# The sixteen gate columns move into the first head's v group, which becomes the second group of the input projection; side streams pause once instead of twice, and a head's loads are issued while the head before it still runs

## The chip, the core and the metric

The kernel runs on one core of a Trainium2 chip. The metric is device time in microseconds (us). The engines are named as in the profile: PE (TensorE), PEld (its weight loads), DVE (VectorE), ACT (ScalarE), POOL (GpSimd), SP (SyncE, which only issues DMAs here). L69 is line 69 of the kernel before.

## The reference, cut to what matters

One encoder block on 512 tokens of width 2048. The first projection feeds two branches, and the sixteen columns `g` of it are the gates of the second branch.

```python
hn = rmsnorm(x, norm1_w[l])
proj = hn @ w_in[l]                              # 2048 -> 11280 columns
conv_out = centred_depthwise_conv(proj[..., :5120], ...)
rest = proj[..., 5120:]
hv, hx1, hx2 = ...                               # 3 x 1024 columns: the hyena branch
z   = hx1 * long_conv(hv, kf[:, 0], hb[0])
y_a = hx2 * long_conv(z, kf[:, 1], hb[1])
q, k = silu(conv_out[..., 3072:])                # 4 heads of 256
v = rest[..., :1024]                             # columns 5120..6143
o = sigmoid(rest[..., 1024:2048])
g = rest[..., 2048:2064] + mlstm_gate_bias[l]    # 16 columns: 4 gates x 4 heads
y_b = o * (mlstm(q, k, v, g forward) + mlstm(q, k, v, g backward))
x = x + (gate_a * (y_a @ w_branch_a) + gate_b * (y_b @ w_branch_b)) @ w_out
x = x + (silu(gate) * up) @ w_down               # the feed-forward part, then a last rmsnorm
```

## The kernel before, in words

Every fp32 product is made of three TensorE passes (`mm3`, L69): an operand is split into a high and a low part (`wh`/`wl` for weights, `a` for the normalised input, `g` for tiles of the side work), by a cast on ACT (L169 for weights) and a subtraction on DVE (L170).

The part that the change touches is the first 840 us or so. It is a **main stream** with **side streams** woven into it. The main stream multiplies the input by `w_in` in groups of 256 columns: a group is 16 blocks of 128 rows, taken two at a time (a unit, 12 matmuls of 512 columns or 24 of 256), and after every unit the generator yields (a tick). Weights come by SP in pieces of four blocks (`load_a`, three buffers); the class `Weights` splits them two units ahead. A q, k or hyena group holds two PSUM banks of the pool `mm` (four banks), a v group (`group_v`) holds all four, since there the input stands still in the array and the weights stream through.

The order of groups in the main stream is written out: the first hyena group; then `gate_cols`, the sixteen gate columns as a group of their own; then the hyena's second and third kinds, hyena part 1, head 0 (q, k, v), hyena parts 2 and 3, heads 1 to 3, and four groups `o`. `gate_cols` puts the gate weights into a 128-column tile `wg` (most of it zero), multiplies it with the input, adds the bias in rows (`gb`) and turns the result by four small matmuls against `csm` into token-major `gates`.

At each tick `drive` gives the side streams 2.6 units of cost, about one for each us of DVE work. `turns` goes round the streams; a stream that yields "pause" is skipped until two ticks later (PAUSE = 2), and one that yields "wait" has nothing to do yet. Stream b makes the filter network and eight filter spectra, then the combinations `T` for the next phase. Stream a starts with `gate_rows` (gate arithmetic on small tiles `gs`), then does hyena 0 and 1, head 0, hyena 2 and 3 and heads 1 to 3 (`mlstm`). A head loads q and k (POOL queue), splits them, makes four score tiles (S, 24 matmuls of 512 columns, evicted by ACT at L861), loads v and a row of decays, and then makes weights on ACT, POOL (`affine_select`, L898) and DVE (L900, L904) for the matmuls `num` of 258 columns. All tiles `g` come from one pool of 24 buffers.

The order of instructions on each engine is then set by a scheduling layer from its own estimates; each engine works its list off in that order.

After this phase come the Winograd groups (tiles `T`), the branches, the output projection and the feed-forward part; the change does not touch their code.

Of the kernel before, what the change touches and what calls it, by code (L numbers as in the profile page):

```python
# [8 lines left out]
F32 = mybir.dt.float32  # L9
# [25 lines left out]
def hybrid_block_kernel(ctx, tc, x, norm1_w, w_in, conv_w, conv_b, filt_w1, filt_b1, filt_freq1,  # L35
# [26 lines left out]
    def mm_ps():  # L62
        return new(pm, "mm")

    def sd_ps():
        return new(psd, "sd")
# [14 lines left out]
        return h, l  # L81


    csm = new(cp, "csm", (P, 3 * P + 16))
    nc.sync.dma_start(csm[:, 0:P], c_small[:, 0:P])
    ident = csm[:, 0:P]
    triu = csm[:, P:2 * P]
    tril = csm[:, 2 * P:3 * P]
    sel32 = csm[0:32, 3 * P:3 * P + 16]
    onesf = new(cp, "onesf", (P, P))  # L90
    nc.vector.memset(onesf, 1.0)

# [63 lines left out]
        return bc  # L156


    def load_a(w, r0, c0, nk=4, ncol=256):
        n_tile[0] += 1  # L160
        raw = wpool[0].tile([P, nk, ncol], F32, tag="wr", name=f"wr_{n_tile[0]}", bufs=3)
        nc.sync.dma_start(raw, w[r0:r0 + nk * P, c0:c0 + ncol].rearrange("(k p) c -> p k c", p=P))
        return raw

    def split_w(src, shape):
# [7 lines left out]
    class Weights:  # L173
# [6 lines left out]
        def get(self, c0, kb):  # L180
            assert self.units[self.given] == (c0, kb)
            while len(self.made) < min(self.given + 1 + self.ahead, len(self.units)):
                uc, uk = self.units[len(self.made)]
                if uk % 4 == 0:
                    self.raw = load_a(w_in, uk * P, uc)
# [211 lines left out]
    def head_cols(h):  # L397
        for base, blk0, dst in ((C_Q, 24, d_q), (C_K, 32, d_k)):
            for r in group_feat(w_in, 0, KB, base + h * 256, X, ahead=ahead):
                if r is None:  # L400
                    yield
            for j in range(2):
                conv_evac(r[j], blk0 + 2 * h + j, False, store_to(dst[2 * h + j]))
        later.append((0, lambda: done.add(("qk", h))))
        for r in group_v(w_in, C_V + h * 256, X, ahead):
            if r is None:
                yield
        for tb in range(4):
# [3 lines left out]
        done.add(("v", h))  # L412

    def o_cols(g):
        for r in group_feat(w_in, 0, KB, C_O + g * 256, X, ahead=ahead):
# [9 lines left out]
    a_col = new(cp, "a_col", (P, 2, 4, 4))  # L425
    em_col = new(cp, "em_col", (P, 2, 4, 4))

    gates_t = []

    def gate_cols():  # L430
        gps = mm_ps()
        for u in range(0, KB, 4):
            raw = load_a(w_in, u * P, C_G, 4, 16)
            n_tile[0] += 1
            g = wp.tile([P, 4, P], F32R, tag="wh", name=f"wg_{n_tile[0]}", bufs=4)
            nc.vector.memset(g.bitcast(F32), 0.0)
# [7 lines left out]
        gb = new(cp, "gb", (32, 1))  # L444
        nc.vector.memset(gb, 0.0)
        nc.gpsimd.dma_start(gb[0:16], mlstm_gate_bias[0].rearrange("g h -> (g h)").rearrange("(n o) -> n o", o=1))
        gT = gt()
        nc.vector.tensor_tensor(gT[0:32], gps[0:32], rbc[0:32], ALU.mult)
        nc.vector.tensor_scalar(gT[0:32], gT[0:32], gb, None, ALU.add)
        ps = sd_ps()  # L450
        for tb in range(4):
            mm(ps[:, tb * 16:(tb + 1) * 16], gT[0:32, tb * P:(tb + 1) * P], sel32, True, True)
        gates = new(cp, "gates", (P, 4, 2, 2, 4))
        gates_t.append(gates)
        nc.vector.tensor_copy(gates.rearrange("p a b c d -> p (a b c d)"), ps[:, 0:64])
        done.add("gates matmul")

    def gate_rows():
        yield from need("gates matmul")
        gates = gates_t[0]  # L460

        n = [0]

        def sm(shape=(P, 32)):
            n[0] += 1
            return pr.tile(list(shape), F32, tag=f"gs{n[0]}", name=f"gs{n[0]}", bufs=1)

        f = sm()
        nc.vector.tensor_copy(f.rearrange("p (d t h) -> p t d h", d=2, t=4), gates[:, :, :, 1, :])
# [76 lines left out]
    def filter_net():  # L546
# [16 lines left out]
        nc.sync.dma_start(csm[:, P:3 * P + 16], c_small[:, P:3 * P + 16])  # L563
        yield "pause"
        for m, t in enumerate(tables):
            hh = new(ph, f"dH{m}", dt=F32R)
# [160 lines left out]
    def conv_long(q, o, halves, finish):  # L727
# [45 lines left out]
        for half in range(2):  # L773
# [7 lines left out]
            finish(half, ps)  # L781
            yield 1.4

    def hyena(q):
        yield from need(("hy", q))

        def load(kind):
            ts = []
            for j in range(2):
                t = gt()  # L790
                nc.gpsimd.dma_start(t, d_hy[kind][2 * q + j])
                ts.append(t)
            return ts

        u = load(0)
        x1 = load(1)
        yield "pause"
        halves = []
        for ps in by_times(u):
# [3 lines left out]
        for ps in by_times(x1):  # L803
            t = gt()
            nc.scalar.copy(t, ps)
            x1t.append(t)
        yield "pause"
        z = []

        def gate(half, ps):  # L810
# [2 lines left out]
            z.append(gsplit(t))  # L813

        yield from conv_long(q, 0, halves, gate)
        x2 = load(2)
        y = []

        def keep(half, ps):
# [1 line left out]
            nc.scalar.copy(t, ps)  # L821
            y.append(t)

        yield "pause"
        yield from conv_long(q, 1, z, keep)
        yield "pause"
        for j in range(2):
# [7 lines left out]
            yield 1.1  # L835


    def mlstm(h):
        yield from need("gates")
        yield from need(("qk", h))  # L840
        qs, ks = [], []
# [6 lines left out]
        yield "pause"  # L848
        for dst in (qs, ks):
            for j in range(2):  # L850
                dst.append(gsplit(raw.pop(0)))
                yield .7
        yield "pause"
        S = []
        for sb in range(4):
# [5 lines left out]
            nc.scalar.activation(t, ps, AF.Copy, scale=1.0 / 16)  # L861
            S.append(t)
            yield .3
        yield from need(("v", h))

        def load_row(d):
            t = gt()
            nc.gpsimd.dma_start(t, d_rows[4 * d + h:4 * d + h + 1].to_broadcast([P, L]))
            return t

        V = []
        raw = []
        for b in range(2):
            t = gt()
            nc.gpsimd.dma_start(t.rearrange("p (b c) -> p b c", b=2),
                                d_v[h][2 * b:2 * b + 2].rearrange("b p c -> p b c"))
            raw.append(t)
        row = load_row(0)
        yield "pause"
# [34 lines left out]
        for n, (d, jb) in enumerate(units):  # L914
            if n == 4:
                W = {}
            W[jb] = nxt
            if n < 7:
                nxt = weights(*units[n + 1], row if n < 3 else row_b)
# [30 lines left out]
            yield "wait"  # L950

    def stream_a():
        yield from gate_rows()
        yield from need("filter")
        for kind, n in (("hy", 0), ("hy", 1), ("hd", 0), ("hy", 2), ("hy", 3)):
            yield from hyena(n) if kind == "hy" else mlstm(n)
        ph_cm.__exit__(None, None, None)
        ts_pool.append(ts_cm.__enter__())
        done.add("ts")
        for h in (1, 2, 3):  # L960
            yield from mlstm(h)

    def stream_b():
        yield from filter_net()
# [162 lines left out]
    N_PLAIN = 4  # L1127
    AHEAD = 2
    RATIO = 2.6
    side = turns(stream_b(), stream_a())  # L1130

    parts = (("hy", 1), ("hd", 0), ("hy", 2), ("hy", 3), ("hd", 1), ("hd", 2), ("hd", 3))
    groups = [HW, 2 * HW]
    for kind, n in parts:
        groups += [b + 256 * n for b in ((0, HW, 2 * HW) if kind == "hy" else (C_Q, C_K, C_V))]
# [403 lines left out]
```

## Time and profile before

| | us |
|---|---|
| median of 3 runs (lowest, highest) | 2893.85 (2893.14, 2894.86) |
| time of the profiled execution | 2894.33 |
| its span, first to last instruction | 2892.3 |
| PE busy over the span | 2864.4 |
| DVE busy over the span | 2107.2 |
| ACT busy over the span | 1274.4 |
| mean granted TensorE clock | 0.998 |

A row of the timeline gives the start, the duration, the engine, the line, the operation with its output and inputs, and how many were merged; a bracket gives idle time before it and what ended it. Matmuls overlap in that view (their ends are modelled), so the cost of one in a row of many is the distance from start to start, and the chain view, which gives each piece only the time that it adds, shows the same. A row of the waits gives who waited for whom, the sum, how often, and the longest.

### The profile page before, as it was taken

What the parts mean: (1) busy time and instruction counts of PE and PEld (TensorE: products, weight loads), DVE (VectorE), ACT (ScalarE), POOL (GpSimd) and SP (SyncE); (2) the same over time, 40 slices, a digit from 0 to 9 for tenths busy, and PEclk for the clock granted to TensorE, in tenths of its full rate; (3) what the DMA queues carried; (4) which work ended last, traced back from release to release, by engine and by line L of the source; (5) the groups of instructions that cost most, each with busy time, mean ns of one, the idle gap of its engine ahead of it and who ended that gap; (6) DMA issues with size and microseconds to landing.
All of it is one profiled execution on the core that took longest, in us unless ns stands there. A gap on an engine that the chain in (4) does not pass through costs nothing.

```text
span 2892.3 us, 48200 instructions
## 1 busy us (share of the span) xinstructions
PE 2864.4 (99%) x18412; PEld 2592.2 (90%) x18412; DVE 2107.2 (73%) x3844; ACT 1274.4 (44%) x2267; POOL 185.7 (6%) x431
## 2 busy tenths in 40 slices
PE   9999999999999999999999999999999999999998
PEld 7788887898889999888899999999999998888886
DVE  7897977889588888454549888888888985233336
ACT  5434354436565455222435444444444445233224
POOL 0101011102210001000110000000000000000000
PEclk9999999999999999999999999999999999999999
DMA  5334334334444444743443433343343336343333
GB/s 179 121 108 130 117 117 141 111 106 143 149 136 128 135 140 138 245 139 95 152 148 109 129 121 114 120 126 118 117 128 114 118 110 207 96 130 117 124 113 127
DMA packets 285589, 377.01 MB, mean 130 GB/s; under 512 B 18620, under 2 KB 222852, under 8 KB 285357
## 3 DMA queue, kind: packets, MB, share of 16 engines
q1 hardware_dynamic: 261339, 298.36, 33.4%
q0 software_dynamic: 22752, 73.44, 7.5%
q8 instruction: 144, 2.36, 0.3%
q10 hardware_dynamic: 1266, 2.13, 0.2%
q14 instruction: 88, 0.72, 0.1%
HBM read 326.67 MB, written 47.20 MB: 129 GB/s over the span
## 4 chain that ended last, share of the span: by engine, by line
PE 94%; DVE 3%; DMA 2%; issue 1%; ACT 1%; SPq 0%; POOL 0%; DVEq 0%; ACTq 0%; POOLq 0%
PE mm L69 67%; PE sd L69 26%; DMA bt<-d_o 1%; DMA wr<-in_w_down_dram 0%; DVE wl L170 0%; DVE st L373 0%; PE sd L288 0%; PE sd L724 0%; PE sd L1302 0%; DVE s L1063 0%; DVE st L370 0%; DMA g<-d_q 0%; DMA xt<-in_x_dram 0%; DVE h L80 0%; DVE T L1330 0%
## 5 line engine op out<-in xcount | busy, mean ns | idle before, releaser
L170 DVE TENSOR_TENSOR wl<-wr,wh 128x512 fp32r<-128x512 f32 x512 | 352.6, 693 | 484.9 <-ACT wh L169 479.0
L169 ACT CAST wh<-wr 128x512 fp32r<-128x512 f32 x512 | 316.5, 621 | 761.5 <-PE mm L69 708.1
L69 PE MATMUL mm<-a,wh 128*128 128x512 f32 (+1 forms) x2128 | 623.2, 376 | 0.0
L69 PEld LDWEIGHTS mm<-a,wh 128*128 128x128 f32 x2128 | 385.0, 189 | 69.2 <-issue 4.1
L69 PE MATMUL mm<-T,wh 128*128 128x256 f32 x2232 | 402.3, 282 | 2.6 <-ACT T L1329 2.2
L69 PE MATMUL mm<-a,wl 128*128 128x512 f32 (+1 forms) x1064 | 398.9, 375 | 1.5 <-DVE wl L170 1.4
L69 PE MATMUL sd<-T,wh 128*128 128x256 f32 x2224 | 399.2, 282 | 0.0
L69 PE MATMUL mm<-wh,h 128*128 128x512 f32 x1280 | 394.4, 389 | 1.1 <-ACT h L79 1.1
L69 PEld LDWEIGHTS mm<-T,wh 128*128 128x128 f32 x2232 | 343.5, 190 | 3.3 <-ACT T L1329 2.5
L69 PEld LDWEIGHTS sd<-T,wh 128*128 128x128 f32 x2224 | 341.5, 189 | 0.0
L1046 ACT CAST wh<-s 128x512 fp32r<-128x512 f32 x365 | 226.4, 621 | 254.6 <-PE sd L69 125.4
L69 PE MATMUL mm<-T,wl 128*128 128x256 f32 x1116 | 313.0, 280 | 0.3 <-DVE wl L1047 0.3
L69 PE MATMUL sd<-T,wl 128*128 128x256 f32 x1112 | 311.5, 280 | 0.0
L69 PEld LDWEIGHTS mm<-wh,h 128*128 128x128 f32 x1280 | 240.3, 188 | 51.3 <-ACT h L79 1.3
L69 PE MATMUL mm<-wh,a 128*128 128x256 f32 (+1 forms) x1152 | 259.8, 319 | 0.0
L1047 DVE TENSOR_TENSOR wl<-s,wh 128x512 fp32r<-128x512 f32 x365 | 250.0, 687 | 11.6 <-ACT wh L1046 9.7
L69 PE MATMUL mm<-wl,h 128*128 128x512 f32 x640 | 249.0, 389 | 0.0
L69 PEld LDWEIGHTS mm<-a,wl 128*128 128x128 f32 x1064 | 200.9, 189 | 37.8 <-DVE wl L170 3.1
L69 PEld LDWEIGHTS mm<-T,wl 128*128 128x128 f32 x1116 | 212.1, 190 | 0.5 <-DVE wl L1047 0.5
L69 PEld LDWEIGHTS sd<-T,wl 128*128 128x128 f32 x1112 | 211.1, 190 | 0.0
L69 PEld LDWEIGHTS mm<-wh,a 128*128 128x128 f32 x1152 | 192.7, 190 | 15.2
L69 PE MATMUL mm<-wl,a 128*128 128x256 f32 (+1 forms) x576 | 183.2, 318 | 0.0
(368 smaller groups left out, 4819.0 us busy)
## 6 DMA issues: line engine op xcount, KB each, us to landing
wr<-in_w_in_dram SPq DMA_DIRECT2D x140, 512.0 KB, 3.9
r<-in_w_gate_up_dram SPq DMA_DIRECT2D x100, 512.0 KB, 3.6
wr<-in_w_down_dram SPq DMA_DIRECT2D x88, 512.0 KB, 3.7
wr<-in_w_gate_up_dram SPq DMA_DIRECT2D x76, 512.0 KB, 3.6
r<-in_w_in_dram SPq DMA_DIRECT2D x36, 512.0 KB, 4.6
wr<-in_w_out_dram SPq DMA_DIRECT2D x32, 512.0 KB, 4.9
d_h<-xo POOLq DMA_DIRECT2D x44, 256.0 KB, 2.6
hl<-d_h SPq DMA_DIRECT2D x44, 256.0 KB, 3.8
```

What stands on the lines that cost most here:

```text
L69: nc.tensor.matmul(o, a, b, start=start, stop=stop)
L169: nc.scalar.copy(h, src)
L170: nc.vector.tensor_tensor(l, src, h.bitcast(F32), ALU.subtract)
L1046: nc.scalar.copy(h, a)
L1047: nc.vector.tensor_tensor(l, a, h.bitcast(F32), ALU.subtract)
```

## The change: what it does

The gate columns no longer form a group. The first head's v group loads 272 columns instead of 256: a second, narrow DMA per piece brings the sixteen gate columns beside the 256 of v, and the split and the matmuls run over 272 columns. That group now stands second in the main stream, right after the first hyena group, and head 0 is left with q and k where it stood. Four small DVE instructions take the gates, already token-major, out of the four PSUM banks. `gate_rows` becomes a side stream of its own with its small tiles inside one buffer `g`; the triangular matrices that it multiplies with get a tile of their own.

In the side streams, two pauses in a row become one: after the second transposes of a hyena part (now two yields of 0.1), before its second convolution, and, for a head whose v is already there, before its v tiles. Such a head loads v and the first row right after the splits of q and k. Heads 1 and 2 load the q and k of the next head while their sixth unit of eight is being made.

```diff
-    def load_a(w, r0, c0, nk=4, ncol=256):
+    def load_a(w, r0, c0, nk=4, ncol=256, extra=False):
+        n = ncol + 16 if extra else ncol
...
+        if extra:
+            nc.sync.dma_start(raw[:, :, ncol:n], w[r0:r0 + nk * P, C_G:C_G + 16].rearrange("(k p) c -> p k c", p=P))
...
-                self.made.append(split_w(self.raw[:, uk % 4:uk % 4 + 2, :], [P, 2, 256]))
+                self.made.append(split_w(self.raw[:, uk % 4:uk % 4 + 2, :], [P, 2, 272 if uc == C_V else 256]))
...
     def group_v(w, c0, act, ahead=None):
+        n = 272 if ahead is not None and c0 == C_V else 256
...
-                    mm3(ps[tb][:, 0:256], aH[:, ts], aL[:, ts], wh[:, k, :], wl[:, k, :],
+                    mm3(ps[tb][:, 0:n], aH[:, ts], aL[:, ts], wh[:, k, :], wl[:, k, :],
...
+        if h:
+            yield from v_cols(h)
+
+    def v_cols(h):
...
             nc.gpsimd.dma_start(d_v[h][tb], y[:, 0:256])
+            if h == 0:
+                nc.vector.scalar_tensor_tensor(gates[:, tb].rearrange("p b c d -> p (b c d)"), r[tb][:, 256:272],
+                                               rstd[:, tb:tb + 1], gbias, ALU.mult, ALU.add)
...
-    def gate_cols():
-        gps = mm_ps()
-        for u in range(0, KB, 4):
-            raw = load_a(w_in, u * P, C_G, 4, 16)
-            g = wp.tile([P, 4, P], F32R, tag="wh", name=f"wg_{n_tile[0]}", bufs=4)
-            nc.vector.memset(g.bitcast(F32), 0.0)
-            nc.vector.tensor_copy(g[:, :, 0:16], raw)
-            nc.vector.tensor_tensor(g[:, :, 16:32], raw, g[:, :, 0:16].bitcast(F32), ALU.subtract)
-            for k in range(4):
-                kb = u + k
-                mm(gps, g[:, k, :], X[kb][0], kb == 0, False)
-                mm(gps, g[:, k, :], X[kb][1], False, kb == KB - 1)
-            yield
...
-        for tb in range(4):
-            mm(ps[:, tb * 16:(tb + 1) * 16], gT[0:32, tb * P:(tb + 1) * P], sel32, True, True)
...
     def hyena(q):
...
-        yield "pause"
+            yield .1
...
-        yield "pause"
         yield from conv_long(q, 1, z, keep)
...
-    def mlstm(h):
-        yield from need("gates")
-        yield from need(("qk", h))
+    def mlstm(h, following=None):
+        yield from need("gates")
+        if h in fetched_qk:
+            raw = fetched_qk.pop(h)
+        else:
+            yield from need(("qk", h))
+            raw = fetch_qk(h)
+            yield "pause"
...
+        early = ("v", h) in done
+        if early:
+            raw = load_v()
+            row = load_row(0)
         yield "pause"
...
-        yield from need(("v", h))
+        if not early:
+            yield from need(("v", h))
+            raw = load_v()
+            row = load_row(0)
+            yield "pause"
...
+            if n == 5 and ("qk", following) in done:
+                fetched_qk[following] = fetch_qk(following)
...
     def stream_a():
-        yield from gate_rows()
...
-    side = turns(stream_b(), stream_a())
+    side = turns(stream_b(), stream_a(), gate_rows())
...
-    groups = [HW, 2 * HW]
+    groups = [C_V, HW, 2 * HW]
...
-        yield from hyena_cols(0, gate_cols())
+        yield from hyena_cols(0, v_cols(0))
```

PE, before, where the gate group ends and the hyena's second group has begun (`mm_570` is the gates' bank, `sd_681` the filter network, `sd_689` the turned gates):

```order
L69 MATMUL mm_570<-a_460,wg_669 128x512
L69 MATMUL mm_570<-a_461,wg_669 128x512
L69 MATMUL sd_681<-g_614,fw_117_608 128x512
L69 MATMUL mm_696<-a_219,wh_700 128x512
...
L69 MATMUL mm_697<-a_218,wl_701 128x512
L69 MATMUL mm_696<-a_250,wh_704 128x512
L69 MATMUL sd_689<-csm_72,g_686 128x16 x4
L69 MATMUL mm_696<-a_251,wh_704 128x512
```

PE, changed, where the widened v group ends (`mm_576` is its fourth bank) and the hyena's second group begins:

```order
L69 MATMUL mm_575<-wh_806,a_461 128x272
L69 MATMUL mm_576<-wh_806,a_456 128x272
L69 MATMUL mm_576<-wl_807,a_456 128x272
...
L69 MATMUL mm_576<-wl_807,a_460 128x272
L69 MATMUL mm_576<-wh_806,a_461 128x272
L69 MATMUL mm_933<-a_214,wh_836 128x512
```

The 32 matmuls on `wg` and the four on `csm` are gone, 192 matmuls of the v group have 272 columns, and nothing stands between that group and the next.

ACT, before, at head 3, from the last score eviction (L861) to the first two weights (L895 exponential, L903 cast; L885 is the cast of v, L421 the sigmoid of an `o` group):

```order
L861 ACTIVATE g_8591<-sd_8584 128x512
L169 CAST wh_8771<-wr_8769 128x512
L885 CAST g_8633<-g_8593 128x2x256
L421 ACT_TABLE_LOAD
L421 ACTIVATE st_8759<-st_8759 128x512
L885 CAST g_8639<-g_8595 128x2x256
L895 ACT_TABLE_LOAD
L895 ACTIVATE g_8647<-g_8597,a_col_560 128x512
L421 ACT_TABLE_LOAD
L421 ACTIVATE st_8763<-st_8763 128x512
L903 CAST g_8651<-g_8647 128x512
```

ACT, changed, at the same place (L878 is the eviction, L892 the cast of v, L902 the exponential, L910 the cast):

```order
L878 ACTIVATE g_8478<-sd_8471 128x512
L892 CAST g_8480<-g_8394 128x2x256
L892 CAST g_8486<-g_8396 128x2x256
L902 ACT_TABLE_LOAD
L902 ACTIVATE g_8494<-g_8398,a_col_560 128x512
L169 CAST wh_8643<-wr_8641 128x512
L169 CAST wh_8702<-wr_8641 128x512
L910 CAST g_8498<-g_8494 128x512
```

The weights now follow the scores at once, with one table load between them instead of three. On PE, 24 matmuls of the main stream stand between the last score matmul and the first `num` of head 3, where 46 stood; at head 2 it is 24 instead of 36, at head 0 41 instead of 49.

POOL, before, around the loads of head 3's q and k (L846; `d_yb` are stores of head 2's result, L875 loads v, L868 the row):

```order
L898 AFFINE_SELECT g_8344<-g_8344 128x128
L898 AFFINE_SELECT g_8380<-g_8380 128x128
L846 DMA g_8465<-d_q_115 128x512
L942 DMA d_yb_149<-g_8454 128x512
L942 DMA d_yb_150<-g_8462 128x512
L846 DMA g_8467<-d_q_116 128x512
L846 DMA g_8469<-d_k_123 128x512
L846 DMA g_8471<-d_k_124 128x512
L875 DMA g_8593<-d_v_136 128x2x256
```

POOL, changed, around the same loads (L832):

```order
L905 AFFINE_SELECT g_8208<-g_8208 128x128
L832 DMA g_8243<-d_q_115 128x512
L832 DMA g_8245<-d_q_116 128x512
L832 DMA g_8247<-d_k_123 128x512
L832 DMA g_8249<-d_k_124 128x512
L905 AFFINE_SELECT g_8251<-g_8251 128x128
L905 AFFINE_SELECT g_8271<-g_8271 128x128
L433 DMA d_o_127<-st_8400 128x512
L433 DMA d_o_128<-st_8404 128x512
L951 DMA d_yb_149<-g_8333 128x512
```

The four loads have moved ahead of head 2's last two selects and of its stores. Over the whole program PE has 3,120 matmuls of the main stream in this phase instead of 3,152, and ACT 16 table loads instead of 23.

More of the change, by code (lines that the diff above doesn't have):

```diff
@@ L81, in split @@
         return h, l
-    csm = new(cp, "csm", (P, 3 * P + 16))
+    csm = new(cp, "csm", (P, P))
     nc.sync.dma_start(csm[:, 0:P], c_small[:, 0:P])
     ident = csm[:, 0:P]
-    triu = csm[:, P:2 * P]
-    tril = csm[:, 2 * P:3 * P]
-    sel32 = csm[0:32, 3 * P:3 * P + 16]
     onesf = new(cp, "onesf", (P, P))
@@ L184, in get @@
                 if uk % 4 == 0:
[L185 to L186 removed]
+                    self.raw = load_a(w_in, uk * P, uc, extra=uc == C_V)
+                self.made.append(split_w(self.raw[:, uk % 4:uk % 4 + 2, :], [P, 2, 272 if uc == C_V else 256]))
             self.given += 1
@@ L411, in head_cols @@
             nc.gpsimd.dma_start(d_v[h][tb], y[:, 0:256])
+            if h == 0:
+                nc.vector.scalar_tensor_tensor(gates[:, tb].rearrange("p b c d -> p (b c d)"), r[tb][:, 256:272],
+                                               rstd[:, tb:tb + 1], gbias, ALU.mult, ALU.add)
         done.add(("v", h))
+        if h == 0:
+            done.add("gates matmul")
     def o_cols(g):
@@ L426, in hybrid_block_kernel @@
     em_col = new(cp, "em_col", (P, 2, 4, 4))
-    gates_t = []
-    def gate_cols():
-        gps = mm_ps()
-        for u in range(0, KB, 4):
-            raw = load_a(w_in, u * P, C_G, 4, 16)
-            n_tile[0] += 1
-            g = wp.tile([P, 4, P], F32R, tag="wh", name=f"wg_{n_tile[0]}", bufs=4)
-            nc.vector.memset(g.bitcast(F32), 0.0)
-            nc.vector.tensor_copy(g[:, :, 0:16], raw)
-            nc.vector.tensor_tensor(g[:, :, 16:32], raw, g[:, :, 0:16].bitcast(F32), ALU.subtract)
-            for k in range(4):
-                kb = u + k
-                mm(gps, g[:, k, :], X[kb][0], kb == 0, False)
-                mm(gps, g[:, k, :], X[kb][1], False, kb == KB - 1)
-            yield
[L444 to L450, printed above, removed]
-        for tb in range(4):
-            mm(ps[:, tb * 16:(tb + 1) * 16], gT[0:32, tb * P:(tb + 1) * P], sel32, True, True)
[L453 to L456, printed above, removed]
+    gates = new(cp, "gates", (P, 4, 2, 2, 4))
+    gbias = new(cp, "gbias", (P, 16))
+    nc.gpsimd.dma_start(gbias, mlstm_gate_bias[0].rearrange("g h -> (g h)").rearrange("(o n) -> o n", o=1)
+                        .to_broadcast([P, 16]))
+    triangles = []
     def gate_rows():
         yield from need("gates matmul")
-        gates = gates_t[0]
+        triu, tril = triangles[0][:, 0:P], triangles[0][:, P:2 * P]
         n = [0]
+        room = gt()
         def sm(shape=(P, 32)):
-            n[0] += 1
-            return pr.tile(list(shape), F32, tag=f"gs{n[0]}", name=f"gs{n[0]}", bufs=1)
+            n[0] += shape[1]
+            return room[:, n[0] - shape[1]:n[0]]
         f = sm()
@@ L562, in filter_net @@
         nc.sync.dma_start(zt[0:33], c_zt)
-        nc.sync.dma_start(csm[:, P:3 * P + 16], c_small[:, P:3 * P + 16])
+        tri = new(pr, "tri", (P, 2 * P))
+        nc.sync.dma_start(tri, c_small[:, P:3 * P])
+        triangles.append(tri)
         yield "pause"
@@ L782, in conv_long, with fetch @@
             yield 1.4
+    def fetch(q, kind):
+        ts = []
+        for j in range(2):
+            t = gt()
+            nc.gpsimd.dma_start(t, d_hy[kind][2 * q + j])
+            ts.append(t)
+        return ts
     def hyena(q):
         yield from need(("hy", q))
[L787 to L796, printed above, removed]
+        u, x1 = fetch(q, 0), fetch(q, 1)
         yield "pause"
@@ L815, in hyena @@
         yield from conv_long(q, 0, halves, gate)
-        x2 = load(2)
+        x2 = fetch(q, 2)
         y = []
@@ L835, in hyena, with fetch_qk @@
             yield 1.1
-    def mlstm(h):
-        yield from need("gates")
-        yield from need(("qk", h))
-        qs, ks = [], []
+    def fetch_qk(h):
         raw = []
@@ L847, in mlstm @@
                 raw.append(t)
-        yield "pause"
+        return raw
+    fetched_qk = {}
+    def mlstm(h, following=None):
[6 more added lines that the diff above has]
+            yield "pause"
+        qs, ks = [], []
         for dst in (qs, ks):
@@ L852, in mlstm, with load_row, load_v @@
                 yield .7
+        def load_row(d):
+            t = gt()
+            nc.gpsimd.dma_start(t, d_rows[4 * d + h:4 * d + h + 1].to_broadcast([P, L]))
+            return t
+        def load_v():
+            raw = []
+            for b in range(2):
+                t = gt()
+                nc.gpsimd.dma_start(t.rearrange("p (b c) -> p b c", b=2),
+                                    d_v[h][2 * b:2 * b + 2].rearrange("b p c -> p b c"))
+                raw.append(t)
+            return raw
+        early = ("v", h) in done
+        if early:
+            raw = load_v()
+            row = load_row(0)
         yield "pause"
@@ L863, in mlstm @@
             yield .3
-        yield from need(("v", h))
[L866 to L869, printed above, removed]
-        V = []
[L872 to L879, printed above, removed]
+        if not early:
[3 more added lines that the diff above has]
+            yield "pause"
+        V = []
         for t in raw:
@@ L960, in stream_a @@
         for h in (1, 2, 3):
-            yield from mlstm(h)
+            yield from mlstm(h, h + 1)
     def stream_b():
@@ L1129, in hybrid_block_kernel @@
     RATIO = 2.6
-    side = turns(stream_b(), stream_a())
+    side = turns(stream_b(), stream_a(), gate_rows())
     parts = (("hy", 1), ("hd", 0), ("hy", 2), ("hy", 3), ("hd", 1), ("hd", 2), ("hd", 3))
-    groups = [HW, 2 * HW]
+    groups = [C_V, HW, 2 * HW]
     for kind, n in parts:
-        groups += [b + 256 * n for b in ((0, HW, 2 * HW) if kind == "hy" else (C_Q, C_K, C_V))]
+        groups += [b + 256 * n for b in ((0, HW, 2 * HW) if kind == "hy" else (C_Q, C_K, C_V) if n else (C_Q, C_K))]
     ahead = Weights(groups + [C_O + 256 * g for g in range(4 - N_PLAIN, 4)], AHEAD)
     def w_in_cols():
-        yield from hyena_cols(0, gate_cols())
+        yield from hyena_cols(0, v_cols(0))
         for part in parts:
```

4 lines of the change are left out of this document (2 added, 2 removed).

## The prediction

> **What bounds the kernel now.** I read the page's first and fourth part, then the waits of PE in the first phase, then the timeline and the chain at the places that the change touches.
>
> ```profile
> PE 2864.4 (99%) x18412; PEld 2592.2 (90%) x18412; DVE 2107.2 (73%) x3844; ACT 1274.4 (44%) x2267; POOL 185.7 (6%) x431
> PE 94%; DVE 3%; DMA 2%; issue 1%; ACT 1%; SPq 0%; POOL 0%; DVEq 0%; ACTq 0%; POOLq 0%
> core 0: 2892.3 us, clock 0.998
> ```
>
> PE is busy for 99% of the span at the full clock, and 94% of the chain that ended last is PE's. So a matmul taken out shortens the time by its own length, unless a wait comes in its place; work on the other engines counts only where PE waits for it. What PE waits for between 40 and 845 us, the part in which the change lies:
>
> ```profile
> PE sd L69 <- ACT g L344: 1.2, 1, 1.2
> PE mm L69 <- DVE wl L170: 1.0, 1, 1.0
> PE sd L69 <- DVE g L677: 0.9, 3, 0.5
> PE sd L724 <- DMA g<-d_hy: 0.8, 1, 0.8
> PE sd L69 <- DVE g L345: 0.5, 1, 0.5
> PE mm L69 <- ACT h L1046: 0.4, 1, 0.4
> PE mm L69 <- DVE l L1047: 0.4, 1, 0.4
> PE sd L69 <- DVE g L449: 0.3, 1, 0.3
> PE sd L69 <- DVE g L904: 0.2, 1, 0.2
> ```
>
> These nine rows add up to 5.7 us. That is all that better timing of the side streams could ever win here; the rest of a gain must come from matmuls that go.
>
> **The change part by part.** First what leaves PE. The timeline where the gate group ends and its result is turned, and the group of all 32 gate matmuls:
>
> ```profile
> 42.15 3.92 PE L69 MATMUL mm<-a,wg 128*128 128x512 f32 x16
> 45.91 0.61 PE L69 MATMUL mm<-a,wh 128*128 128x512 f32 x2
> ...
> 46.81 1.98 PE L69 MATMUL mm<-a,wg 128*128 128x512 f32 x8
> 48.72 1.12 PE L69 MATMUL sd<-g,fw 33*128 33x512 f32 x2
> ...
> 52.38 1.03 PE L69 MATMUL sd<-csm,g 32*128 32x16 f32 x8 [0.26 <-DVE g L449]
> 53.34 0.50 PE L69 MATMUL mm<-a,wh 128*128 128x512 f32 x1
> ...
> L69 PE MATMUL mm<-a,wg x32: 387/390/486, 39.4 to 48.4; 128*128 128x512 f32 x32
> ```
>
> From start to start 16 of them take 45.91 - 42.15 = 3.76 us and 8 take 48.72 - 46.81 = 1.91 us, so 24 take 5.67 us, 0.236 us each (the 390 ns in the last row overlap). Thirty-two are 7.5 us. The four turning matmuls take 53.34 - 52.38 = 0.96 us and PE waited 0.26 us for them: 1.2 us. Together 8.7 us go.
>
> What comes is 16 more columns in 192 matmuls (16 blocks, four token tiles, three passes). A v group of before is 256 wide, the other groups 512; the chain gives 48 of each, and the timeline has a batch of 258 columns:
>
> ```profile
> 249.40 5.84 PE mm L69 x48
> 735.71 10.90 PE mm L69 x48
> ...
> 772.45 1.61 PE L69 MATMUL sd<-g,g 128*128 128x258 f32 x12
> 773.90 0.39 PE L69 MATMUL mm<-a,wh 128*128 128x512 f32 x1
> ```
>
> That is 0.1217 us for 256 columns and 0.2271 us for 512, so a straight line gives 0.0066 us for 16 columns and 192 x 0.0066 = 1.3 us. Below it could be nothing, since 258 columns cost (773.90 - 772.45)/12 = 0.121 us, no more than 256; above, in proportion to the width, 192 x 0.0076 = 1.5 us. I take 1.3.
>
> The v group fills all four banks, and the hyena group behind it needs the first two of them at once. Until now only ACT emptied such banks; now a DVE instruction of 16 columns must also have read each, and DVE works in the order of its list, with full-width operations between those four. No row shows that wait. At best it is 0; at worst two operations of the length of L900 below (0.69 us) stand ahead: 1.4 us. I take 0.3, since the last matmuls of the group, on the other two banks, run meanwhile for 12 x 0.128 = 1.5 us.
>
> The narrow loads: four of 32 KB were there before for the gate tile, and four are there now, each behind a 512 KB piece of the v group.
>
> ```profile
> wr<-in_w_in_dram SPq DMA_DIRECT2D x16, 512.0 KB, 3.6
> ...
> wr<-in_w_in_dram SPq DMA_DIRECT2D x2, 32.0 KB, 2.0
> ```
>
> One piece and its narrow load, one after the other, are 5.6 us; PE needs 48 x 0.128 = 6.1 us for the four blocks that they hold, and three buffers run ahead. So I take 0, and at worst one exposed landing, 2.0 us. [...]
>
> Head 3's scores. Before, head 3's q landed late, and PE stood for it:
>
> ```profile
> 787.77 4.99 DMA g<-d_q
> ...
> 794.49 6.05 PE L69 MATMUL sd<-g,g 128*128 128x512 f32 x24 [1.18 <-ACT g L344]
> ```
>
> The loads are now issued before head 2's last two weights, so they no longer end that wait. Next late is ACT: between head 2's last transposes and the scores only 13 main matmuls are left (13 x 0.227 = 3.0 us) for two evictions and four casts of about 0.6 us on ACT, 3.6 us. So 0.6 us of waiting stays and 0.6 us goes (between 0 and 1.2).
>
> From the scores to the first `num`, at heads 2 and 3, only 24 main matmuls are left: 24 x 0.227 = 5.45 us. What must fit is seen at head 2 before:
>
> ```profile
> 752.20 0.60 ACT L861 ACTIVATE g<-sd 128x512 f32<-128x512 f32 x1 [0.78 <-PE sd L69]
> ...
> 755.26 1.14 ACT L885 CAST g<-g 128x512 fp32r<-128x512 f32 x2
> 756.41 1.28 ACT L895 ACT_TABLE_LOAD   x1
> 757.71 0.72 ACT L895 ACTIVATE g<-g,a_col 128x512 f32<-128x512 f32 x1
> ...
> 758.83 0.69 DVE L900 TENSOR_TENSOR g<-g,g 128x512 f32<-128x512 f32 x1 [1.54 <-POOL g L898]
> ...
> 759.56 0.62 ACT L903 CAST g<-g 128x512 fp32r<-128x512 f32 x1 [0.61 <-DVE g L900]
> ...
> 760.23 1.83 PE L69 MATMUL sd<-g,g 128*128 128x258 f32 x12
> ```
>
> From the last eviction to `num` it was 760.23 - 752.20 = 8.0 us, but the casts of v started 755.26 - 752.80 = 2.5 us after ACT was free, behind a weight cast that waited for PE. In the new order none stands there, so 8.0 - 2.5 = 5.5 us must fit into 5.45 us, and the third matmul needs a low part that comes some 0.7 us later. I take 0.3 us of wait for each of the two heads, 0.6 us; at best 0, at worst the old length stays, (8.0 - 5.45) x 2 = 5.2 us. [...]
>
> The early loads of q and k stand on POOL ahead of the last two selects of a head and wait for tiles `g` that `num` matmuls of the fourth unit give back. The two selects, and with them the last two weights, are queued behind. They serve units three further on, so I take 0.2 us; at worst 1 us at each of two heads.
>
> The single pauses take two ticks (24 x 0.227 = 5.5 us) of cover away at eight places, and leave two. What must fit into these before a second convolution is a product, a cast and a subtraction of 0.69 + 0.62 + 0.69 = 2.0 us. I take 0. Of the 5.7 us above, 4.2 us belong to none of the terms before; their places shift, so half of it may go (-2) or as much again may come (+4). The earlier mlstm loads, the table loads and `gate_rows` as a third stream change what lies on ACT, DVE and SP; PE covers it, and where the cover goes it is part of these bounds.
>
> The sum: -7.5 - 1.2 + 1.3 + 0.3 - 0.6 + 0.6 + 0.2 = -6.9 us. The profiled execution took 2894.33 us, 2.0 us more than its span and 0.5 us above the median of the three runs; against the median that is 2893.85 - 6.9 = **2886.9 us**. All lower ends together give -8.7 - 1.2 - 2 = -11.9, 2882; all upper ends -8.7 + 1.5 + 1.4 + 2 + 5.2 + 2 + 4 = +7.4, 2901.
>
> **The rivals.** A measurement of this kernel tells about 0.2%, 5.8 us, from no change: faster ends at 2888.1, slower begins at 2899.6.
>
> *DVE becomes the bound and hands the time back.* The first stretches after the gates:
>
> ```profile
> 40.00:60.00 20.00, 19.74 (x89) 15.04 (x88) 18.64 (x41) 7.92 (x12) 2.88 (x8) 1.00 0.59 186
> 60.00:80.00 20.00, 19.95 (x93) 15.53 (x92) 18.87 (x59) 8.51 (x14) 0.00 (x0) 1.00 0.20 60
> 80.00:100.00 20.00, 19.77 (x87) 14.33 (x86) 18.62 (x39) 7.59 (x12) 1.92 (x7) 1.00 0.34 100
> 100.00:120.00 20.00, 20.00 (x109) 17.07 (x108) 17.98 (x39) 7.15 (x12) 5.41 (x13) 1.00 0.62 204
> L436 DVE MEMSET wg<- x4: 485/485/485, 29.7 to 39.3; 128x512 f32 x4
> ```
>
> The fourth column is DVE: 74.1 of 80 us. If PE gives up 7.4 us here and DVE only the four memsets (1.9 us), DVE stands at 72.2 of 72.6 us, and PE would begin to wait: some 4 us back, 2891. Against it: the side streams get their work per tick, and four ticks go with the gate group, so 4 x 2.6 = 10.4 us of DVE work move behind this stretch.
>
> *The weights of heads 2 and 3 stay late.* The worst of that term, 5.2 instead of 0.6 us: 2891.5. For it speaks that only 5.45 us of cover are left, against it that one table load stands there instead of three. With it I count the narrow load exposed (2.0 us, 2889).
>
> *Slower: the single pauses expose DVE.* At eight places PE reaches the next transforms 5.5 us sooner. The chain there is 2.0 us, so nothing shows until DVE is more than 3.5 us behind its list; from then on each us is lost at each place. To end slower it takes 6.9 + 5.8 = 12.7 us, 1.6 us at each, a DVE 5.1 us late: 2900 and more. The stretches above, with DVE at 93%, speak for it; that PE waited 0.5 us in all for those splits (L345) speaks against it.
>
> **How the numbers follow.** The forecast has 0.70; about 0.08 of it lies above 2888.1. DVE as the bound 0.14, late weights or loads 0.10, exposed pauses 0.06. So faster is 0.62, same 0.08 + 0.14 + 0.10 = 0.32, slower 0.06. The range reaches from the lower ends, 2882, past the two rivals around 2891 to 2892.5; outside lie the slower rival and about a tenth more.
>
> **What would show it.** No matmul on `wg`; 48 matmuls of 272 columns in about 6.1 us in the chain; a wait at the head of the hyena's second group below 1 us; no wait behind the landing of head 3's q; waits of PE on L911 or L910 (the split weights) of some tenths at heads 2 and 3; the sum of PE's waits from 40 to 840 us between 4 and 8 us, and the phase's end some 7 us earlier. I am wrong if that sum grows past 10 us, above all by waits for DVE in the first 300 us or after a first convolution, or if 272 columns cost a step more than the line gives.

## The result, and the profile after

| | before | after |
|---|---|---|
| median, us (lowest to highest) | 2893.56 (2893.14 to 2894.86) | 2913.29 (2913.0 to 2913.89) |
| ratio, 95% interval | | 1.0068, 1.0056 to 1.0079 |
| span of the profiled execution, us | 2892.3 | 2911.5 |

The change made the kernel 19.7 us slower; the forecast was 6.9 us faster. The kernel before was measured again beside each set of runs, at medians of 2893.56 to 2894.30 us; every ratio below is to the one of its own set. From the page of after:

```profile
PE 2882.9 (99%) x18372; PEld 2597.3 (89%) x18372; DVE 2111.5 (73%) x3832; ACT 1265.5 (43%) x2260; POOL 185.8 (6%) x431
core 0: 2911.5 us, clock 0.997
```

PE has 40 instructions fewer and is busy 18.5 us longer, at nearly the same clock (0.997 after 0.998). What PE waits for between 40 and 830 us:

```profile
PE sd L716 <- DMA g<-d_hy: 0.8, 1, 0.8
PE mm L69 <- DVE pp L366: 0.5, 1, 0.5
PE sd L69 <- ACT g L346: 0.4, 1, 0.4
PE sd L69 <- DVE g L347: 0.4, 1, 0.4
PE sd L69 <- DVE g L911: 0.4, 1, 0.4
PE sd L69 <- DVE g L480: 0.3, 1, 0.3
```

That is 2.8 us; the rows of before in the same stretch come to 4.9. Where the change lies the waits have shrunk. The loss is in code that the change doesn't touch. The chain at the end of the first phase, of before and of after (start, us, what):

```profile
840.46 0.69 DVE s L1063
...
842.40 14.03 PE mm L69 x116
```

```profile
834.70 3.26 DMA d_o<-st
...
838.66 1.29 DVE s L1071 x2
...
842.51 16.23 PE mm L69 x120
```

The Winograd stage begins no earlier than before, since its first combination `s` (a DVE sum of weights) waited for a store `d_o` out of the old ring `st`; and its first 120 matmuls take 16.23 us, where 14.03 x 120 / 116 = 14.5 would be the old pace (the granted clock is 0.83 from 840 to 850 us). Further on many matmuls are slower at the full clock (1.00 from 1530 to 2400 us). Groups of 168 matmuls in the second Winograd stage, and the timeline of the down-projection, before first:

```profile
1606.06 19.88 PE mm L69 x168
...
2463.91 0.39 PE L69 MATMUL mm<-wl,h 128*128 128x512 f32 x1
2464.59 0.39 PE L69 MATMUL mm<-wl,h 128*128 128x512 f32 x1
```

```profile
1611.88 20.04 PE mm L69 x168
...
2464.28 0.40 PE L69 MATMUL mm<-wl,h 128*128 128x512 f32 x1
2464.98 0.39 PE L69 MATMUL mm<-wl,h 128*128 128x512 f32 x1
2465.68 0.40 PE L69 MATMUL mm<-wl,h 128*128 128x512 f32 x1
...
2469.15 0.39 PE L69 MATMUL mm<-wl,h 128*128 128x512 f32 x1
2469.83 0.39 PE L69 MATMUL mm<-wl,h 128*128 128x512 f32 x1
```

From one of these rows to the next PE runs three 512-column matmuls: 0.68 us throughout before, 0.70 in half of each group after and 0.68 in the other half. The slow half is always the same half, and PE waits for nothing there. It goes with the buffer: the weights stand in a ring of four slots, and the two slots at one residue are slow. What the change did to them is not in its diff as such: a tag's slots are as large as its widest tile, so `wh` and `wl` slots grew from 2048 to 2176 bytes for the whole program. Byte addresses in a partition modulo 256, from the two programs, and matmuls counted by whether the moving operand starts at the same address modulo 256 as the stationary operand of the next one:

```
                                       before          after
wh, wl, the four slots                 0 0 0 0         224 96 224 96
a (input), h (down-projection)         0               224
T, first Winograd stage                0               224
T, second Winograd stage               224, some 0     224
y (branches)                           224             224
512 columns: equal / unequal           5319 / 634      2957 / 2964
256 columns: equal / 224 / 128 apart   5106 / 5603 / - 7035 / - / 4388
end of the ring st / start of s        178112 / 178144 178304 / 178144
```

Sorted in this way over both traces, a 512-column matmul behind the first phase takes about 226.7 ns from start to start with equal addresses and about 233 unequal; one of 256 columns 119.9 equal, 118.4 with 128 and 118.1 with 224 apart. In what follows a pair is a matmul's moving operand and the next one's stationary operand, and it is equal when both start at the same address modulo 256. Theory A: the addresses make the loss, with the overlap of `st` and `s` in the last row of the table. Rivals: the changed order of work with its waits and contention (B), the clock (C).

### The profile page after: what moved, and what is told of

Same layout as the page of the kernel before. It is cut to its first block, busy times and chain, and to the rows that moved or that the text cites. A ratio compares the mean times of both kernels' runs of the same rounds, so it can differ in the third digit from the quotient of the medians.

```text
span 2911.5 us, 48126 instructions
## 1 busy us (share of the span) xinstructions
PE 2882.9 (99%) x18372; PEld 2597.3 (89%) x18372; DVE 2111.5 (73%) x3832; ACT 1265.5 (43%) x2260; POOL 185.8 (6%) x431
## 4 chain that ended last, share of the span: by engine, by line
PE 69%; issue 1%; DVE 1%; DMA 1%; ACT 0%; POOL 0%; POOLq 0%; ACTq 0%; DVEq 0%
PE mm L69 49%; PE sd L69 21%; DMA wr<-in_w_down_dram 0%; PE sd L1310 0%; DVE s L1071 0%; DVE h L80 0%; DVE T L1338 0%; DMA d_o<-st 0%; ACT h L79 0%; POOL d_o L433 0%; DVE wl L170 0%; ACT h L1054 0%; DVE wl L1055 0%; POOL d_yb L951 0%; DVE x L1474 0%
## 5 line engine op out<-in xcount | busy, mean ns | idle before, releaser
L170 DVE TENSOR_TENSOR wl<-wr,wh 128x512 fp32r<-128x512 f32 (+1 forms) x512 | 351.3, 690 | 464.2 <-ACT wh L169 461.2
L169 ACT CAST wh<-wr 128x512 fp32r<-128x512 f32 (+1 forms) x512 | 316.2, 620 | 752.9 <-PE mm L69 692.2
L69 PE MATMUL mm<-wh,a 128*128 128x256 f32 (+2 forms) x1152 | 262.2, 320 | 0.5 <-DVE pp L366 0.5
L69 PE MATMUL mm<-wl,a 128*128 128x256 f32 (+2 forms) x576 | 184.1, 320 | 0.0
```

What stands on the lines that cost most here:

```text
L69: nc.tensor.matmul(o, a, b, start=start, stop=stop)
L169: nc.scalar.copy(h, src)
L170: nc.vector.tensor_tensor(l, src, h.bitcast(F32), ALU.subtract)
```

## The experiments

**e1: only a shift.** The kernel before and 128 unused bytes.

```diff
     wp = ctx.enter_context(tc.tile_pool(name="wp", bufs=1))
+    new(ctx.enter_context(tc.tile_pool(name="pad", bufs=1)), "pad", (P, 32))
```

> The kernel before, not one instruction changed: an unused tile of 128 bytes per partition stands between the ring of split weights (wh, wl) and all tiles that are allocated behind it from the left (a, h, hl, T of the first Winograd stage). Theory A, addresses: a 512-column matmul takes about 226.7 ns from start to start where the moving operand and the next stationary operand start at the same address modulo 256 bytes, and about 233 ns where they don't; 256-column matmuls lose nothing or win about 1 ns by it. Before has 5319 equal and 634 unequal 512-column pairs, here 241 and 5712: 5078 x 6.2 ns = 31 us more, less some 4 us at the 256-column ones, so +27 us, about 2921 (2915 to 2927). Theory B, the loss comes from what the change does to the order of work, to waits or to contention between engines: nothing of that is touched, so 2893.5 within 2 us. Theory C, a lower granted clock (0.997 against 0.998): 2893.5 as well.

Measured: 2916.25 us (2915.58 to 2917.81), ratio to before 1.0079 (1.0062 to 1.0096), clock 0.998. Its group of the down-projection (line numbers are one higher for the added line):

```profile
L70 PE MATMUL mm<-wh,h 128*128 128x512 f32 x1280 | 401.4, 395 | 1.1 <-ACT h L80 1.1
```

The mean duration in that group was 389 ns in the kernel before and is 395 ns here, and 22 us came from a shift alone, at the full clock. B and C fall as explanations of slower matmuls. The size was estimated 5 us too high: in the first phase, where side matmuls stand between, equal pairs took about 227.9 ns (before) and unequal ones 232.8 (e1), 4.9 instead of 6.2 ns apart.

**e2: the ring's addresses put straight in the changed kernel.**

```diff
+    def slot(tag, shape):
+        i = taken[tag] % 4
+        taken[tag] += 1
+        t = wp.tile([P, 544], F32R, tag=f"{tag}{i}", name=f"{tag}_{n_tile[0]}", bufs=1)
+        size = math.prod(shape[1:])
+        at = 32 if tag == "wl" and size < 544 else 0
+        t = t[:, at:at + size]
...
-        h = wpool[0].tile(shape, F32R, tag="wh", name=f"wh_{n_tile[0]}", bufs=WB[0])
-        l = wpool[0].tile(shape, F32R, tag="wl", name=f"wl_{n_tile[0]}", bufs=WB[0])
+        h = slot("wh", shape)
+        l = slot("wl", shape)
...
+        if tag in taken:
+            return slot(tag, shape)
```

> The changed kernel with its work and order; only the ring of split weights is laid out in another way: eight slots of 2176 bytes as in the change, but a 256-column tile of wl starts 128 bytes into its slot, so that all wh and wl tiles start at the same address modulo 256, which is also that of a, h, y and T. Theory A, addresses: 512-column pairs with unequal addresses fall from 2964 to 231, 2733 x 6.2 ns = 17 us less; 4388 256-column pairs become equal, which was 119.9 against 118.4 ns, 6.6 us more: 2913.3 - 17 + 6.6 = 2903 (2898 to 2907), the down-projection back to 226.7 ns a matmul throughout. Theory B, order, waits, contention: 2913 within 2 us. Theory C, clock: 2913.

Measured: 2905.25 us (2903.61 to 2906.34), ratio 1.0039 (1.0024 to 1.0054): 8 us back, within theory A's range. The second Winograd stage, whose 256-column pairs are all equal now, takes 897.5 us from its first matmul to the down-projection, against 893.3 in after and 885.4 in before.

**e3 and e6: TensorE alone.** Two kernels of nothing but matmuls, all other engines idle.

```diff
+            nc.tensor.matmul(ps[i % 4][:, 0:n], st[i % 2][:, ds // 4:ds // 4 + P],
+                             mv[i // 2 % 2][:, dm // 4:dm // 4 + n], start=True, stop=True)
```

> Nothing of the reference is computed: 120 matmuls to warm up, then 132 blocks of 24 matmuls without any other engine at work, f32r, two moving and two stationary tiles in turn, four banks. Blocks go over 512, 256 and 128 columns, the stationary operand 0, 32, 64, 128 bytes and the moving one 0, 16, 32, 64, 96, 128, 160, 192, 224, 256, 384 bytes past a common address modulo 256. Theory A, the two reads of TensorE meet at some addresses: 512 columns take about 227 ns where the offsets are equal modulo 256 and about 233 ns elsewhere, 256 columns about 119.9 and 117 to 119. Theory B, other engines' traffic is what slows: no difference between blocks.

> Nothing of the reference is computed: a finer sweep of TensorE alone, f32r, in the order of the kernel (two moving operands for one stationary one, then another; 12 matmuls into a bank). 256 columns with both operands at every multiple of 32 bytes modulo 256, once row by row with 36 matmuls and once column by column in reverse with 24, the moving operand 256 bytes further with the stationary one at 0, and 512 columns over the same 64 pairs. Theory A, the pair of addresses sets the time: both sweeps give each pair the same time, 256 bytes further changes nothing, and 512 columns are at 227 ns on the diagonal and near 233 off it. If the time depends on the blocks ahead as well, the two sweeps differ. For 256 columns some pairs at 113.3 ns as in the first sweep, others up to 120.

Measured, mean ns from start to start within a block, by how far the moving operand starts past the stationary one modulo 256 (the second sweep with the stationary operand at 0; the other seven rows repeat it along the diagonal, but for single blocks):

```
bytes past            0      32     64     96     128    160    192    224
512 columns         227.8  233.4  228.9  233.7  233.3  234.4  233.3  233.3
256, row by row     120.0  117.8  117.8  119.8  118.7  117.3  113.3  118.3
256, by column      120.0  116.7  117.8  120.0  118.9  118.8  113.3  118.3
256, 256 bytes on   120.0  117.8  117.8  119.6  118.6  117.5  113.3  118.1
```

In the first sweep a moving operand 16 bytes further gave 231.6 ns at 512 columns, 256 further 227.2 and 384 further 233.4; with 128 columns every block stood at 111.5 to 111.8. So the pair of addresses sets most of the pace with no other engine at work, its period is 256 bytes, and the two widths want different things: 512 columns want 0, 256 columns want 192. The 113.3 ns lie outside the 117 to 119 that e3 expected. Something beside the pair has a smaller say: at 160 bytes the two orders of e6 differ by 1.5 ns, 2 of its 16 blocks at 192 bytes stood near 117.8, and one block at 64 bytes in e3 took 113.5. By where the other operand lies a 512-column matmul took 227.8 or 233.4 ns with nothing else at work. That the two reads of TensorE meet, as theory A of e3 has it, is the author's guess; what in the chip does it, no run shows.

**e4: the old addresses with the new work.** As e2, and:

```diff
+    new(cp, "pad", (P, 24))
...
-    gates = new(cp, "gates", (P, 4, 2, 2, 4))
-    gbias = new(cp, "gbias", (P, 16))
+    gates = new(pr, "gates", (P, 4, 2, 2, 4))
+    gbias = new(pr, "gbias", (P, 16))
```

> The changed kernel with all its work and order, laid out so that its tiles have the addresses modulo 256 of the kernel before: wl tiles 128 bytes into their slots as in the run before, the gates' tile and their bias moved to the pool of the first phase, and 96 unused bytes at the front. Pairs of 512 columns equal/unequal: 5317/604 (before 5319/634); of 256 columns equal 4931, 224 apart 5608 (before 5106, 5603). Theory A, addresses: the whole 20.7 us by which matmuls of unchanged shape became slower goes; left are the prediction's terms, -6.9, and the new wait of 3 to 4 us where the Winograd stage begins: 2890 (2886 to 2892). Theory B, that the change itself slows the later stages: above 2905.

Measured: 2892.21 us (2890.79 to 2893.0, 11 executions), ratio 0.9993 (0.9984 to 1.0002). 21.1 us of the loss are the addresses. The time is 0.2 us above the upper end of A's range: the wait at the Winograd stage is still there, and it cost more than the 3 to 4 us that were allowed for it. Its chain, what PE waited for there (3.0 and 1.5 us are the longest of each row), and slices around it (us, busy time of PE, PEld, DVE, ACT, POOL, granted clock):

```profile
828.85 3.46 DMA d_o<-st
...
832.40 0.70 DVE s L1083
...
836.39 18.23 PE mm L69 x130
```

```profile
PE mm L69 <- ACT wh L1066: 3.5, 2, 3.0
PE mm L69 <- DVE wl L1067: 1.8, 2, 1.5
```

```profile
830.00:840.00 10.00, 5.49 (x31) 5.08 (x30) 6.86 (x12) 4.13 (x7) 0.00 (x0) 0.76 0.07 24
840.00:850.00 10.00, 10.00 (x78) 10.00 (x78) 8.68 (x15) 4.00 (x7) 0.00 (x0) 0.90 0.58 182
835.20:842.00 6.80, 5.61 (x26) 5.62 (x27) 6.80 (x12) 3.13 (x6) 0.00 (x0) 0.50 0.00 0
```

**e7: the overlap taken away.** Against e4:

```diff
-        tri = new(pr, "tri", (P, 2 * P))
+        tri = new(pr, "tri", (P, 2 * P + 40))
...
-    gates = new(pr, "gates", (P, 4, 2, 2, 4))
+    gates = new(ph, "gates", (P, 4, 2, 2, 4))
```

> The run with the old layout once more (2892.2 us), but the pool of the first phase is 160 bytes larger at its end and the gates' tile and bias lie in another pool, so that the ring st ends at byte 178144 of a partition, where the first tile s of the Winograd stage begins; in the changed kernel, as in that run, the third st slot reaches 160 bytes into s. Theory A: the wait of 4.8 us where the Winograd stage begins comes from that overlap (the first s cannot be written before the last store out of st has landed), so it goes, with the dip of the clock behind it, and what the change really does to the work is seen: 2892.2 - 4 - 1 = 2887.5 (2886 to 2889), which is also the prediction's own sum. Theory B: DVE or the loads of the first Winograd weights are late for another reason: 2892 within 1.5.

Measured: 2886.23 us (2885.22 to 2887.93, 9 executions), ratio 0.9975 (0.9965 to 0.9984). Its chain at the same place, and the slices:

```profile
830.14 1.29 DVE s L1083 x2
...
835.09 14.04 PE mm L69 x116
```

```profile
830.00:840.00 10.00, 9.00 (x71) 8.40 (x71) 9.91 (x18) 4.85 (x9) 0.00 (x0) 1.00 0.21 69
840.00:850.00 10.00, 10.00 (x86) 10.00 (x85) 9.56 (x19) 4.53 (x8) 0.54 (x1) 1.00 0.53 171
```

The store is gone from the chain, the clock stays at 1.00, and the piece of 116 matmuls that began at 842.40 in the kernel before begins at 835.09. A 160-byte overlap of two rings cost 6.0 us: 3.5 in waits (3.0 + 1.5 = 4.5 us at that place in e4, not the 4.8 of the expectation; 1.0 here), and 18.23 - 14.04 x 130 / 116 = 2.5 us in the clock, which was granted at 0.50 from 835.2 to 842.0 us in e4. What length of wait brings that about, no run settles.

**e5 and e8: one half of the change each.** e5 is e4 with the side streams of before, e8 is the kernel before with the new side streams. Two of e5's edits against e4 (it also takes the early loads back):

```diff
-    side = turns(stream_b(), stream_a(), gate_rows())
+    side = turns(stream_b(), stream_a())
...
-            yield .1
+        yield "pause"
```

> The run before this one with the side streams of the kernel before: double pauses, every load where it stood, gate_rows at the head of the first stream. Only the gates' columns ride in the v group, and that comes second. Tests the prediction's first terms alone, -7.5 - 1.2 + 1.3 + 0.3 = -7.1 us. Theory A: 2886.5 (2884 to 2889) if the new wait at the start of the Winograd stage comes from the side streams; about 2890 if it comes from the gate group's going.

> The kernel before with the side streams of the change alone: single pauses, gate_rows as a third stream, the early loads. The gate group stays where it was, and so do all addresses of TensorE's operands. Theory A, TensorE's own instructions set the time and the side streams only have to end in time: 2894 within 2 us, and the streams run out earlier, with less DVE and ACT work in the last 40 us of the first phase. Theory B, the single pauses expose DVE: 2897 or more.

Measured: e5 2918.5 us (2918.37 to 2919.1), ratio 1.0084 (1.0071 to 1.0098), a clear miss of the expectation; e8 2893.71 us (2891.49 to 2894.8), ratio 0.9998 (0.9989 to 1.0007). The waits of e5, and its chain after the last main matmul:

```profile
PE sd L69 <- ACT g L907: 10.7, 6, 5.5
PE mm L69 <- ACT wh L1050: 8.2, 2, 7.6
```

```profile
832.35 5.17 PE sd L69 x22
837.52 2.75 issue
840.29 0.29 POOL g L902
840.60 0.70 DVE g L904
841.32 0.63 ACT g L907
841.99 4.48 PE sd L69 x19
...
854.66 2.33 DMA d_yb<-g
857.24 3.45 DMA r<-in_w_in_dram
```

With the gate group's four ticks gone and the old side streams still there, the last head is not done when the main stream ends; its weights go from POOL to DVE to ACT to PE with nothing beside them, and only then come the loads for the Winograd stage. In e8 the streams end early: DVE is busy for 24.9 of the 40 us from 800 to 840 instead of 31.4, ACT 17.4 instead of 31.3, and nothing is won. So the new side streams are worth nothing alone and 2918.5 - 2892.2 = 26.3 us once the gate group is gone, a part of it by the clock (0.992 on average in e5, 0.996 in e4). How much of that the single pauses are worth, and how much the early loads and the third stream, no run separates.

**e9 and e10: the layout that the sweeps ask for.** T 192 bytes past its weights, y equal to its weights; e9 with the code of before, e10 on e7. Only unused bytes are added, in e10 also some small tiles moved to make room for them. From e9:

```diff
+    def pad_pool(name, size, **where):
+        cm = tc.tile_pool(name=name, bufs=1, reuse_waits="tile", **where)
+        new(cm.__enter__(), name, (P, size // 4))
+        return cm
...
+        ts_pool.append(pad_pool("pad_ts", 192))
...
+    pad_py = pad_pool("pad_py", 224, side="right")
...
+    pad_w2 = [pad_pool("pad_t2", 192)]
```

> The kernel before, with no instruction changed; only unused bytes in front of some pools, so that the Winograd stages' moving operand T starts 192 bytes past its stationary operands modulo 256 (8582 of the 256-column pairs) and y starts like the weights it meets (512 columns). By the sweep 192 bytes apart give 113.3 ns, 224 or 0 apart, as these pairs stand in the kernel before, 118.3 and 120.0: 5544 x 4.8 ns + 3000 x 5.9 ns + 384 x 6.5 ns = 47 us. Theory A: about 2848 (2840 to 2865). Theory B, that the sweep's figure doesn't carry over, since weight loads fill TensorE in the Winograd stages: above 2885.

> The changed kernel with the same layout as the run before this one: wh, wl, a, h and y start at one address modulo 256, T 192 bytes past it, and st ends where s begins. Theory A: the 2887.5 us of the run without the overlap less the 47 us of the addresses, about 2841 (2833 to 2858), and some 7 us below the kernel before with the same layout. Theory B as there: above 2880.

Measured: e9 2849.99 us, ratio 0.9848 (0.9833 to 0.9864); e10 2844.32 us, ratio 0.9857 (0.9815 to 0.9900). Theory A holds for both: 44 us were gained in e9, where 47 were expected, and e10 is 5.7 us below e9, where some 7 were. A group of 168 matmuls of e10 in the second Winograd stage, and its group on y; then the group on y of before:

```profile
1626.77 19.04 PE mm L69 x168
...
L69 PE MATMUL mm<-y,wh 128*128 128x512 f32 x256 | 78.7, 389 | 0.0
```

```profile
L69 PE MATMUL mm<-y,wh 128*128 128x512 f32 x256 | 80.5, 396 | 0.0
```

One of five executions of e9 took 2881.1 us and one of four of e10 2876.9. The slower one of e9 is the one that was profiled: there the 256-column matmuls of the second Winograd stage run at 113.5 ns until 1531 us, pass a short interruption by other matmuls (`csm` against `rb`, from 1528.3 us), and then stay at 117.8 ns for 850 us. That the slower execution of e10 is of the same kind is likely, but it was not traced. The same group of 168 in e9:

```profile
1636.65 19.79 PE mm L69 x168
```

## Why the prediction was wrong, point by point

The mechanism of the change was right, and e7 shows its size: -7.9 us against the kernel before in the same session, where the sum gave -6.9. What failed is the step before the sum: that the time differs only by what is removed, added, moved and waited for. All terms were taken from the first 840 us; that the code behind them keeps its pace was never written down as a term and has none in the range. It cost 21.1 us by addresses (after less e4) and 6.0 us by the overlap (e4 less e7): -7.9 + 27.1 = +19.2, measured 19.7. These are steps from run to run, so they must add up, but for 0.5 us between sets of runs. The size of the largest is borne out apart from them: a shift alone cost 22 us (e1), and an estimate from the counts gives 2330 more unequal pairs of 512 columns at 4.9 to 6.3 ns, 11 to 15 us, and 893.3 - 885.4 = 7.9 us in the second Winograd stage, 19 to 23 us in all.

- *The gate matmuls and the four turning matmuls, -8.7.* Right in kind: the same piece of 116 Winograd matmuls starts 842.40 - 835.09 = 7.3 us sooner in e7.
- *272 columns, +1.3.* Eight triples in e7, 24 matmuls, take 50.57 - 47.58 = 2.99 us:

```profile
47.58 0.41 PE L69 MATMUL mm<-wh,a 128*128 128x272 f32 x2
...
50.57 0.41 PE L69 MATMUL mm<-wh,a 128*128 128x272 f32 x2
```

  That is 0.1246 us each, 0.0029 above the 0.1217 that the prediction took for 256 columns, so 0.6 us for 192. Against the 119.9 ns of a 256-column matmul with equal addresses it is 0.0047, 0.9 us. Either way it is less than 1.3. The tiles of 272 columns also start at other addresses, so what the width alone costs is not shown.
- *The slots of the wider tiles* were not seen at all. The prediction followed the sixteen columns through DMA, cast and matmul, and not the tag's slot size, which all groups up to the end of the program share. This is the term that decided.
- *PSUM banks of the v group, +0.3.* No wait of PE stands between 66 and 74 us in after or e7: 0.
- *Head 3's q and k, -0.6.* The wait of 1.2 us for ACT on L344 is gone whole: between 605 and 837 us PE waits for nothing in after. The 0.4 us for that cast (L346 in the rows of after) stand at 604.6 us, at a transform of a hyena part. Right in kind, half in size.
- *Scores to num at heads 2 and 3, +0.6.* No wait at either head: 0, the best case of the term. The row on L911 has 0.4 us at 426.8 us, among the `num` matmuls of head 0, for which there was no term.
- *The early loads, +0.2.* No row: 0.
- *The single pauses, 0.* Right for the change as a whole, and in part by luck: the new side streams alone change nothing (e8), but with the old ones the gate group's going makes the kernel 26.3 us slower (e5 less e4). "PE covers it" holds only as long as the main stream has ticks left; the prediction spoke of the 10.4 us of DVE work that move behind, and did not ask whether they still fit before the main stream's end.
- *The rivals.* DVE as the bound: between 40 and 130 us PE waited for it 0.3 us (L480). Late weights, exposed narrow loads, exposed pauses: from 40 us up to the Winograd stage no wait is longer than 0.9 us in after or e7. The slower outcome came by none of the mechanisms that were named for it.
- *The signs of error.* The sum of PE's waits did not pass 10 us and 272 columns cost no step, so both signs of being wrong stayed away while the time was wrong. They looked only at the phase of the change. A sign of being right did fail: the phase's end was to come some 7 us earlier, and the Winograd piece of after begins at 842.51 us against 842.40, behind a wait of 3.2 us for the first weights of that stage.

The waits from 40 to 830 us fell from 4.9 us to 3.2 in e7. With -8.7 and +0.6 this makes -9.8, where -7.3 to -7.9 were measured: about 2 us are not assigned. That the sum of -6.9 came so near to the -7.9 of e7 is therefore in part luck.

## What to carry to other kernels

Before costing a change, list what it does to the places of tiles that it doesn't use: a wider tile in a shared ring, a smaller constant or a moved pool shifts every operand allocated behind it, and can let two rings overlap whose lifetimes then wait for each other. When a time moves, compare the pace of unchanged matmuls late in the program first; if it differs with the same clock and no waits, look at addresses and not at the schedule. Work that is hidden beside a main stream is hidden only up to that stream's last tick; here the edit that shortened the main stream needed the new side streams with it.

## What the runs showed of the hardware that was not expected

- The start addresses of the moving and the stationary operand, modulo 256 bytes, set the pace of f32r matmuls that each load new weights: 512 columns 226.7 ns equal, 228.9 with the moving one 64 bytes further, mostly 233 to 234 at the other multiples of 32; 256 columns 113.3 ns at 192 bytes, 120.0 equal, 116.7 to 120.0 between; 128 columns 111.7 throughout.
- Without any change of an instruction this was worth 22 us of loss (e1) and 44 us of gain (e9) in a kernel of 2894 us.
- At 192 bytes there are two paces, 113.3 and 117.8 ns. In both traces a stream of matmuls without interruption stayed in the one in which it started, at 117.8 for 850 us in the profiled execution of e9 and at 113.3 for 800 us in that of e10; in the second sweep 2 of 16 blocks at that distance stood near 117.8. What chooses between them is open.
- Two waits of PE, 3.0 and 1.5 us with two matmuls between them, cost 2.5 us more afterwards: the clock was granted at 0.50 from 835.2 to 842.0 us (e4).
